# Two heads at a time in three attentions of a two-block transformer kernel: one head per half of the array, probabilities divided before the value product

## The chip, the cores and the metric

The kernel runs on one core of a Trainium2 chip. The metric is the device time of one execution in microseconds. Three runs of the kernel before took 2606.26, 2607.33 and 2609.94 us; the median is 2607.33 us. The core has a matrix engine (PE, with its weight loads shown apart as PEld), three engines for elementwise work (DVE, ACT and POOL), and queues that move data between the memory outside and the on-chip memory. PE writes into PSUM, which this kernel divides into eight tiles of 128 partitions by 512 fp32 values, called banks here.

## The reference

512 tokens of width 1024 pass through a first block of one layer and a second block of two layers. Each layer mixes tokens by several branches and then applies a feed-forward network. Three attentions matter here.

The first block has a sliding-window attention with 8 query heads of width 64 that share 2 key-value heads; a query sees the 128 latest keys, and a learned sink value is added to each denominator:

```python
scores = jnp.einsum('bnqhgd,bnkhd->bnhgqk', qb, kw)
logits = jnp.where(valid[None, :, None, None], scores + alibi, -jnp.inf)
m = jnp.maximum(logits.max(axis=-1), sink)
p = jnp.exp(logits - m[..., None])
denom = p.sum(axis=-1) + jnp.exp(sink - m)
o = jnp.einsum('bnhgqk,bnkhd->bnqhgd', p, vw) / jnp.moveaxis(denom, 4, 2)[..., None]
```

Each layer of the second block has an attention with 8 heads of width 64 in which a query sees only the 128 keys that an index picks. The index scores come from 4 heads of width 64; the bias of keys not chosen is a large negative number, and the rest is a plain softmax:

```python
rel = jax.nn.relu(jnp.einsum('bqhd,bsd->bqhs', qib.astype(jnp.float32), ki32))
score = jnp.einsum('bqh,bqhs->bqs', wib.astype(jnp.float32), rel)
_, idx = lax.top_k(score, topk)
logits = jnp.einsum('bqhd,bqkhd->bhqk', qb.astype(jnp.float32), k_sel) * scale
p = jax.nn.softmax(logits, axis=-1)
return jnp.einsum('bhqk,bqkhd->bqhd', p, v_sel).astype(q.dtype)
```

Beside each attention runs a chunked linear recurrence with 4 heads of width 128, and its output is merged with that of the attention.

## The kernel before

Activations are held as features by tokens: 8 tiles of 128 features by 512 tokens. A projection (`project`, lines 181 to 196) multiplies weight tiles of 128 by 128 with those tiles. Weights and activations are split into a high and a low part, so each weight tile takes three matmuls of 512 columns: lines 193, 194 and 195. In the profile their output is called mm. For each set of weights, one DMA, a cast on ACT (whi) and a subtraction on DVE or POOL (wlo) go ahead.

The other matmuls, whose output is called at, are plain fp32, and each is two PE instructions in the trace, except for a transpose, which is one. They write into PSUM banks of a lane: lane "a" (the attentions) and lane "h" (the recurrences) have two banks each (`BANKS`), and a tile takes the next bank of its lane when what lay there has been read.

The instruction order of each engine is not the order of the code. A scheduler takes what is ready by its own estimate of the times, so projection matmuls of the stages behind stand between the steps of an attention and of a recurrence head. Once placed, the order of an engine's queue is fixed; on DVE and ACT an instruction that waits holds up those behind it.

The window attention is `swa`. For each of the 4 query blocks of 128 tokens (n), it makes the scores of 8 heads with two PSUM tiles per four heads (line 552); a score product uses the 64 rows (partitions) in which its head lies, rows 0 to 63 or 64 to 127, and streams 256 keys (128 in the first block). DVE adds the bias and finds the maximum (line 558). For each pair of heads ACT takes the exponential and the sum (line 572), PE transposes the probabilities (line 575), ACT copies them (sPT, line 577), and PE multiplies them with the values (line 581): the transposed probabilities are the 128 by 128 stationary operand, 64 columns of values are streamed, and the output is tokens by features, all heads in one PSUM tile o. At the end of the block DVE multiplies by the reciprocal of the denominator (son, line 587), four transposes turn it to features by tokens (line 588, in the profile L239 of a helper), and `split_into` (lines 215 to 218) writes the high part on ACT and the low part on DVE.

The top-k attention is `dsa`. `select` computes index scores of four heads (line 867), weights and sums them, and finds the 128 largest of each row on DVE. `attend(i)` handles the query block i against i + 1 key blocks: for each of 8 heads one score product (line 917), bias and maximum (line 919), exponential (line 921), transposes (line 925), copy (aPT, line 927) and value products (line 929), all in tile o of the block; then the multiplication by the reciprocal (aon, line 933), four transposes and `split_into`. Since o stays for the whole block, scores and transposed probabilities share the other bank of the lane.

The recurrence heads (`hgrn_head`) run beside it in lane "h": level by level DVE and POOL update hf and hG, make lvx, and PE multiplies (lines 502 and 457).

## Time and profile before

| | |
|---|---|
| three runs, us | 2606.26, 2607.33, 2609.94 |
| profiled execution: span, us | 2605.2 |
| mean granted clock of PE | 0.993 of full speed |
| PE busy, us (share) | 2533.9 (97%) |
| PE weight loads, us (share) | 2040.0 (78%) |
| DVE busy, us (share) | 1355.5 (52%) |
| ACT busy, us (share) | 1000.8 (38%) |
| POOL busy, us (share) | 754.3 (29%) |

The page gives no other time of the profiled execution than its span, from its first to its last instruction. PE counts as busy while any matmul is in it, and matmuls overlap: one of 512 columns lasts 0.39 us by the trace, and the next starts 0.23 us after it. So a busy share near 100% does not show what an instruction really occupies; that is read from the distance between the starts.

### The profile page before, as it was taken

What the parts mean: (1) busy time and instruction counts of PE and PEld (TensorE: products, weight loads), DVE (VectorE), ACT (ScalarE), POOL (GpSimd) and SP (SyncE); (2) the same over time, 40 slices, a digit from 0 to 9 for tenths busy, and PEclk for the clock granted to TensorE, in tenths of its full rate; (3) what the DMA queues carried; (4) which work ended last, traced back from release to release, by engine and by line L of the source; (5) the groups of instructions that cost most, each with busy time, mean ns of one, the idle gap of its engine ahead of it and who ended that gap; (6) DMA issues with size and microseconds to landing.
All of it is one profiled execution on the core that took longest, in us unless ns stands there. A gap on an engine that the chain in (4) does not pass through costs nothing.

```text
span 2605.2 us, 31523 instructions
## 1 busy us (share of the span) xinstructions
PE 2533.9 (97%) x11742; PEld 2040.0 (78%) x11742; DVE 1355.5 (52%) x2568; ACT 1000.8 (38%) x1813; POOL 754.3 (29%) x640
## 2 busy tenths in 40 slices
PE   9999999999999997999999999999799999999999
PEld 7777888788888865777878888887577787888887
DVE  4565322477774579675244444336967524444432
ACT  5543333444443333553343333334354433433321
POOL 4234334511101234443351111013545435211100
PEclk9999999999999999999999999999899999999999
DMA  3112222222222221111322222322110122222232
GB/s 135 57 51 81 93 94 93 101 97 96 97 94 90 90 73 65 42 41 51 99 96 94 97 95 94 96 88 81 65 49 33 45 94 97 97 97 97 95 101 87
DMA packets 67434, 217.66 MB, mean 84 GB/s; under 512 B 7744, under 2 KB 8640, under 8 KB 67280
## 3 DMA queue, kind: packets, MB, share of 16 engines
q1 hardware_dynamic: 67280, 215.65, 24.9%
q8 instruction: 92, 1.51, 0.2%
q14 instruction: 62, 0.51, 0.1%
HBM read 213.52 MB, written 2.10 MB: 83 GB/s over the span
## 4 chain that ended last, share of the span: by engine, by line
PE 83%; DVE 12%; issue 2%; POOL 2%; ACT 1%; DMA 0%; SPq 0%; DVEq 0%; POOLq 0%; ACTq 0%
PE mm L194 24%; PE mm L195 24%; PE mm L193 24%; PE at L917 1%; PE mm L169 1%; PE mm L168 1%; PE mm L170 1%; DVE score L879 1%; PE at L929 1%; DVE m L878 1%; DVE wlo L152 1%; PE at L239 1%; DVE hf L490 1%; DVE rope L792 1%; DVE rsq_w L232 1%
## 5 line engine op out<-in xcount | busy, mean ns | idle before, releaser
L149 ACT CAST whi<-wraw 128x512 fp32r<-128x512 f32 (+3 forms) x824 | 502.2, 610 | 1177.7 <-PE mm L195 992.1
L194 PE MATMUL mm<-xl,whi 128*128 128x512 f32 x1920 | 757.2, 394 | 0.0
L193 PE MATMUL mm<-xh,wlo 128*128 128x512 f32 x1920 | 756.8, 394 | 0.0
L195 PE MATMUL mm<-xh,whi 128*128 128x512 f32 x1920 | 755.5, 393 | 0.0
L152 DVE TENSOR_TENSOR wlo<-wraw,whi 128x512 fp32r<-128x512 f32 (+1 forms) x529 | 387.4, 732 | 457.9 <-ACT whi L149 455.2
L152 POOL TENSOR_TENSOR wlo<-wraw,whi 128x512 fp32r<-128x512 f32 (+2 forms) x295 | 383.6, 1301 | 767.0 <-ACT whi L149 747.1
L194 PEld LDWEIGHTS mm<-xl,whi 128*128 128x128 f32 x1920 | 361.7, 188 | 79.8 <-issue 7.5
L195 PEld LDWEIGHTS mm<-xh,whi 128*128 128x128 f32 x1920 | 361.6, 188 | 78.2 <-issue 5.6
L193 PEld LDWEIGHTS mm<-xh,wlo 128*128 128x128 f32 x1920 | 361.5, 188 | 76.6 <-issue 3.5
L193 PE MATMUL mm<-acth,wlo 128*128 128x512 f32 x528 | 208.6, 395 | 0.0
L195 PE MATMUL mm<-acth,whi 128*128 128x512 f32 x528 | 208.6, 395 | 0.0
L194 PE MATMUL mm<-actl,whi 128*128 128x512 f32 x528 | 208.6, 395 | 0.0
L725 POOL TENSOR_TENSOR fg<-fg,rstd 128x512 f32<-128x512 f32 x44 | 56.7, 1289 | 426.1 <-ACT fg L724 426.1
L168 PE MATMUL mm<-wlo,xh 128*128 128x512 f32 (+2 forms) x384 | 146.6, 382 | 20.0 <-POOL wlo L152 12.4
L170 PE MATMUL mm<-whi,xh 128*128 128x512 f32 (+2 forms) x384 | 144.5, 378 | 0.0
L169 PE MATMUL mm<-whi,xl 128*128 128x512 f32 (+2 forms) x384 | 144.2, 375 | 0.2 <-DVE xl L281 0.2
L202 DVE TENSOR_TENSOR gate<-mm,rstd 128x512 f32<-128x512 f32 x56 | 38.7, 691 | 169.3 <-PE mm L195 169.3
L270 POOL TENSOR_TENSOR acc<-acc,sq 128x512 f32<-128x512 f32 x39 | 58.7, 1506 | 205.9 <-ACT sq L267 204.9
L195 PEld LDWEIGHTS mm<-acth,whi 128*128 128x128 f32 x528 | 99.0, 187 | 24.3
L193 PEld LDWEIGHTS mm<-acth,wlo 128*128 128x128 f32 x528 | 99.0, 187 | 24.2
L194 PEld LDWEIGHTS mm<-actl,whi 128*128 128x128 f32 x528 | 99.0, 187 | 24.2
L168 PEld LDWEIGHTS mm<-wlo,xh 128*128 128x128 f32 x384 | 73.5, 191 | 40.7 <-POOL wlo L152 15.7
(347 smaller groups left out, 3288.3 us busy)
## 6 DMA issues: line engine op xcount, KB each, us to landing
wraw<-in_w_ffn_in SPq DMA_DIRECT2D x88, 512.0 KB, 3.2
wraw<-in_w_gate SPq DMA_DIRECT2D x56, 512.0 KB, 3.2
wraw<-in_w_in SPq DMA_DIRECT2D x52, 512.0 KB, 3.2
wraw<-in_w_up SPq DMA_DIRECT2D x44, 512.0 KB, 3.2
wraw<-in_w_tok SPq DMA_DIRECT2D x32, 512.0 KB, 3.2
wraw<-in_w_ffn_out SPq DMA_DIRECT2D x32, 512.0 KB, 3.5
wraw<-in_w_down SPq DMA_DIRECT2D x16, 512.0 KB, 3.5
wraw<-in_w_po SPq DMA_DIRECT2D x32, 256.0 KB, 2.6
```

Of the source, the lines that this page charges most:

```text
L149: nc.scalar.copy(wh, raw[:, k:k + m, :])
L152: eng.tensor_tensor(wl, raw[:, k:k + m, :], wh.bitcast(F32), op=OP.subtract)
L168: nc.tensor.matmul(ps[t][:, 0:w], xh, wl, start=i == 0, stop=False)
L169: nc.tensor.matmul(ps[t][:, 0:w], xl, wh, start=False, stop=False)
L170: nc.tensor.matmul(ps[t][:, 0:w], xh, wh, start=False, stop=i == KD - 1)
L193: nc.tensor.matmul(ps, wl, xh, start=i == 0, stop=False)
L194: nc.tensor.matmul(ps, wh, xl, start=False, stop=False)
L195: nc.tensor.matmul(ps, wh, xh, start=False, stop=i == n - 1)
L202: self.nc.vector.tensor_tensor(out, ps, other, op=OP.mult)
L232: nc.vector.scalar_tensor_tensor(w, w, -0.5, y, op0=OP.mult, op1=OP.mult)
L270: (nc.vector if d % 2 and len(acc) > 1 else nc.gpsimd).tensor_tensor(a, a, sq, op=OP.add)
L725: nc.gpsimd.tensor_tensor(g, g, self.rstd, op=OP.mult)
```

## The change

The scores of two heads, one in rows 0 to 63 and one in rows 64 to 127, are issued one behind the other into two PSUM tiles, in `select` and `attend`; `swa` had that already. The reciprocal of the denominator is taken for each pair of heads, and the probabilities are multiplied by it before they are transposed. The value product changes its operands' roles in a new function `values_of`: 64 columns of values are the stationary operand, 128 columns of transposed probabilities are streamed, and the output is features by tokens, one head in output partitions 0 to 63 and the other in 64 to 127 of a PSUM tile that a pair has for itself. It goes to `split_into` at once; the multiplication of the output and its four transposes are left out.

```diff
@@ swa
-            o = self.at([P, 8, 64])
             for h2 in (0, 4, 2, 6):
-                pt = self.at([P, 2, 2, P])
+                dn = den[:, h2:h2 + 2]
                 for s in range(2):
                     hd = h2 + s
                     nc.scalar.activation(Ls[hd], Ls[hd], AF.Exp, scale=-1.0,
                                          bias=nm[:, hd:hd + 1], accum_out=den[:, hd:hd + 1])
+                nc.vector.tensor_tensor(dn, dn, es[:, h2:h2 + 2], op=OP.add)
+                nc.vector.reciprocal(dn, dn)
+                pt = self.at([P, 2, 2, P])
+                for s in range(2):
+                    hd = h2 + s
+                    nc.vector.tensor_scalar(Ls[hd], Ls[hd], den[:, hd:hd + 1], None, op0=OP.mult)
                     for kb in range(w // P):
                         nc.tensor.transpose(pt[:, s, kb, :], Ls[hd][:, kb * P:(kb + 1) * P], self.ident)
                 PT = self.u("sPT", shape=[P, 2, 2, P])
                 nc.scalar.copy(PT[:, :, 0:w // P, :], pt[:, :, 0:w // P, :])
-                for s in range(2):
...
-            nc.vector.tensor_tensor(den, den, es, op=OP.add)
-            nc.vector.reciprocal(den, den)
-            on = self.u("son", shape=[P, 8, 64])
-            nc.vector.tensor_tensor(on, o, den[:, :, None].to_broadcast([P, 8, 64]), op=OP.mult)
-            ps = self.transpose4(on.rearrange("p n c -> p (n c)"), None)
-            for m in range(4):
-                self.split_into(y[m], ps[:, m, :], slice(n * P, (n + 1) * P))
+                kv = slice(P + 64 * (h2 // 4), P + 64 * (h2 // 4) + 64)
+                self.values_of(y[h2 // 2], slice(n * P, (n + 1) * P), w // P, lambda s, kb: (
+                    skv[n + 1 - w // P + kb][:, kv], PT[:, s, kb, :]))
         return y
+
+    def values_of(self, y, c, n, operands):
+        o = self.at([P, P])
+        for kb in range(n):
+            for v in range(2):
+                lhs, rhs = operands(v, kb)
+                self.nc.tensor.matmul(o[64 * v:64 * v + 64, :], lhs, rhs, start=kb == 0, stop=kb == n - 1)
+        self.split_into(y, o, c)
@@ attend
+            for m in range(4):
+                ps = [self.at() for _ in range(2)]
+                L = [self.u("aL") for _ in range(2)]
+                for v in range(2):
+                    r = slice(64 * v, 64 * v + 64)
+                    nc.tensor.matmul(ps[v][:, 0:w], qT[i][r, m, :], kT[m][r, 0:w], start=True, stop=True)
+                for v in range(2):
+                    hd = 2 * m + v
+                    nc.vector.tensor_tensor_reduce(L[v][:, 0:w], ps[v][:, 0:w], bias[i][:, 0:w], -1.0, 3e38,
+                                                   op0=OP.add, op1=OP.min, accum_out=nm[:, hd:hd + 1])
+                    nc.scalar.activation(L[v][:, 0:w], L[v][:, 0:w], AF.Exp, scale=-1.0, bias=nm[:, hd:hd + 1],
+                                         accum_out=den[:, hd:hd + 1])
+                nc.vector.reciprocal(den[:, 2 * m:2 * m + 2], den[:, 2 * m:2 * m + 2])
+                PT = []
+                for v in range(2):
+                    hd = 2 * m + v
+                    nc.vector.tensor_scalar(L[v][:, 0:w], L[v][:, 0:w], den[:, hd:hd + 1], None, op0=OP.mult)
+                    pt = self.at([P, NT, P])
+                    for kb in range(i + 1):
+                        nc.tensor.transpose(pt[:, kb, :], L[v][:, kb * P:(kb + 1) * P], self.ident)
+                    PT.append(self.u("aPT", shape=[P, NT, P]))
+                    nc.scalar.copy(PT[v][:, 0:i + 1, :], pt[:, 0:i + 1, :])
+                self.values_of(y[m], slice(i * P, (i + 1) * P), i + 1, lambda v, kb: (
+                    av[kb][:, P * m + 64 * v:P * m + 64 * v + 64], PT[v][:, kb, :]))
```

In `select` the four index scores are issued in two pairs in the same way. What the scheduler makes of it is seen in the instruction orders. A row of them is a source line, the operation, output and operands by name, and the shape of the output, with a count.

The first place is PE at the second query block of the window attention (L552 scores, L575 and L580 transposes of the probabilities, L239 son those of the output, L593 value products of the change). Before:

```order
L239 MATMUL at<-csts,son 128x128 x4
L552 MATMUL at<-sk,sq 128x256 x2
L193 MATMUL mm<-xh,wlo 128x512
L194 MATMUL mm<-xl,whi 128x512
L195 MATMUL mm<-xh,whi 128x512
L193 MATMUL mm<-xh,wlo 128x512
L194 MATMUL mm<-xl,whi 128x512
L195 MATMUL mm<-xh,whi 128x512
L552 MATMUL at<-sk,sq 128x256 x4
L193 MATMUL mm<-xh,wlo 128x512
L552 MATMUL at<-sk,sq 128x256 x2
L575 MATMUL at<-csts,sL 128x128 x4
```

The same place in the change, on PE:

```order
L593 MATMUL at<-sPT,skv 64x128 x2
L552 MATMUL at<-sk,sq 128x256 x4
L194 MATMUL mm<-xl,whi 128x512
L552 MATMUL at<-sk,sq 128x256 x4
L195 MATMUL mm<-xh,whi 128x512
```

The eight scores stood in groups of 2, 4 and 2 and now stand in two groups of 4; the transposes of the output are gone.

The second place is PE in the top-k attention of the first layer, at two neighbouring steps of the second query block (L917 and L924 scores, L925 and L938 transposes, L929 and L593 value products). Before, one head:

```order
L925 MATMUL at<-csts,aL 128x128 x2
L195 MATMUL mm<-xh,whi 128x512
L193 MATMUL mm<-xh,wlo 128x512
L194 MATMUL mm<-xl,whi 128x512
L929 MATMUL at<-av,aPT 128x64 x2
L917 MATMUL at<-kT,qT 128x256
L195 MATMUL mm<-xh,whi 128x512
```

In the change, a pair of heads, on PE:

```order
L938 MATMUL at<-csts,aL 128x128 x2
L195 MATMUL mm<-xh,whi 128x512
L938 MATMUL at<-csts,aL 128x128 x2
L193 MATMUL mm<-xh,wlo 128x512
L593 MATMUL at<-aPT,av 64x128
L194 MATMUL mm<-xl,whi 128x512
L593 MATMUL at<-aPT,av 64x128 x3
L924 MATMUL at<-kT,qT 128x256
L195 MATMUL mm<-xh,whi 128x512
L193 MATMUL mm<-xh,wlo 128x512
L924 MATMUL at<-kT,qT 128x256
```

Of the four value products the first stands apart from the other three, and two projection matmuls stand between the two scores of the next pair.

The third place is DVE in the same attention of the change (L935 multiplies the probabilities, L931 is the reciprocal, L218 evicts the output of a pair, L490, L486 and L504 belong to a recurrence head):

```order
L931 RECIPROCAL aden<-aden 128x2
L486 TENSOR_TENSOR lvx<-hf,hq 128x32x8
L935 TENSOR_SCALAR aL<-aL,aden 128x256 x2
L490 TENSOR_TENSOR hf<-hf 128x32x8
L486 TENSOR_TENSOR lvx<-hf,hq 128x16x16
L504 COPY_PREDICATED AT<-masks,at 120x32x8
L490 TENSOR_TENSOR hf<-hf 128x16x16
L486 TENSOR_TENSOR lvx<-hf,hq 128x8x32
L218 TENSOR_TENSOR yal<-at,yah 128x128
```

The reciprocal and the multiplies are new between the steps of the recurrence, and the eviction of a pair's output stands behind five of these steps.

## Rows read from the trace of the kernel before

**Rows 1.** The page: busy time by engine, and the chain that ended last.

```profile
PE 2533.9 (97%) x11742; PEld 2040.0 (78%) x11742; DVE 1355.5 (52%) x2568; ACT 1000.8 (38%) x1813; POOL 754.3 (29%) x640
...
PE 83%; DVE 12%; issue 2%; POOL 2%; ACT 1%; DMA 0%; SPq 0%; DVEq 0%; POOLq 0%; ACTq 0%
```

**Rows 2.** Stretches: length, busy time (instructions) by engine, clock, DMA share, GB/s.

```profile
100.00:150.00 50.00, 48.05 (x300) 39.43 (x299) 30.84 (x101) 26.00 (x72) 8.93 (x9) 1.00 0.13 44
...
1100.00:1150.00 50.00, 49.73 (x297) 38.58 (x296) 36.88 (x89) 24.24 (x49) 26.56 (x32) 1.00 0.09 33
1500.00:1550.00 50.00, 50.00 (x222) 41.43 (x221) 22.01 (x33) 17.45 (x28) 5.39 (x5) 1.00 0.28 95
```

**Rows 3.** Timeline of PE, top-k attention: start, length (us), line, names, shapes, count.

```profile
1105.55 0.61 PE L239 MATMUL at<-csts,aon 128*128 128x128 f32 x4
1106.08 0.91 PE L917 MATMUL at<-kT,qT 64*128 64x384 f32 x2
1106.92 0.50 PE L194 MATMUL mm<-xl,whi 128*128 128x512 f32 x1
1107.26 0.40 PE L195 MATMUL mm<-xh,whi 128*128 128x512 f32 x1
1107.49 0.39 PE L193 MATMUL mm<-xh,wlo 128*128 128x512 f32 x1
```

**Rows 4.** Timeline of PE, products with 64 output columns.

```profile
1112.15 0.68 PE L457 MATMUL at<-lvx 128*64 128x64 f32 x8
1112.76 0.50 PE L195 MATMUL mm<-xh,whi 128*128 128x512 f32 x1
1113.09 0.39 PE L193 MATMUL mm<-xh,wlo 128*128 128x512 f32 x1
```

**Rows 5.** Timeline of PE, scores of the window attention.

```profile
78.88 0.71 PE L552 MATMUL at<-sk,sq 64*128 64x128 f32 x8
...
106.44 1.13 PE L552 MATMUL at<-sk,sq 64*128 64x256 f32 x4
...
109.31 1.14 PE L552 MATMUL at<-sk,sq 64*128 64x256 f32 x8
```

**Rows 6.** Timeline of PE, value products of the window attention and what follows.

```profile
97.12 1.00 PE L581 MATMUL at<-skv,sPT 128*128 128x64 f32 x8
97.95 0.61 PE L575 MATMUL at<-csts,sL 128*128 128x128 f32 x4
```

**Rows 7.** Groups by line, PE: count, busy us, mean ns, idle before.

```profile
L929 PE MATMUL at<-av,aPT 128*128 128x64 f32 x320 | 46.0, 275 | 0.0
L581 PE MATMUL at<-skv,sPT 128*128 128x64 f32 x112 | 14.9, 273 | 0.0
L457 PE MATMUL at<-lvx 128*64 128x64 f32 x96 | 8.3, 232 | 5.2 <-POOL lvx L440 3.5 <-DVE lvx L486 1.6
L239 PE MATMUL at<-csts,aon 128*128 128x128 f32 x32 | 4.9, 275 | 0.0
```

**Rows 8.** Groups by line and shape, DVE.

```profile
L933 DVE TENSOR_TENSOR aon<-at,aden 128x512 f32<-128x512 f32 x8 | 5.5, 682 | 2.4 <-PE at L929 2.4
L524 DVE TENSOR_SCALAR alibi<-csts 128x256 f32<-128x256 f32 x8 | 1.7, 286 | 0.0
L931 DVE RECIPROCAL aden<-aden 128x8 f32<-128x8 f32 x8 | 1.6, 202 | 2.5 <-ACT aL L921 2.5
L880 DVE TENSOR_SCALAR score<-score 128x512 f32<-128x512 f32 x2 | 0.9, 428 | 0.1
L749 DVE TENSOR_SCALAR angn<-ang 128x128 f32<-128x128 f32 x2 | 0.4, 222 | 0.0
```

**Rows 9.** Waits of PE: who waited for whom, us in total, times, longest.

```profile
PE at L239 <- DVE aro L817: 20.0, 8, 8.4
PE at L502 <- DVE lvx L486: 2.5, 5, 0.8
PE at L917 <- DVE yal L218: 1.6, 2, 1.0
```

More of the change, by code (lines that the diff above doesn't have):

```diff
@@ L863, in select @@
             sc = self.t("score")
-            for h in range(4):
-                r = slice(64 * (h % 2), 64 * (h % 2) + 64)
-                ps = self.at()
-                nc.tensor.matmul(ps[:, 0:w], iqT[i][r, h // 2, :], ikT[r, 0:w], start=True, stop=True)
-                rl = self.u("rel")
-                nc.scalar.activation(rl[:, 0:w], ps[:, 0:w], AF.Relu)
-                iwc = iw[:, i * 4 + h:i * 4 + h + 1]
-                if h == 0:
-                    nc.vector.tensor_scalar(sc[:, 0:w], rl[:, 0:w], iwc, None, op0=OP.mult)
-                else:
-                    nc.vector.scalar_tensor_tensor(sc[:, 0:w], rl[:, 0:w], iwc, sc[:, 0:w], op0=OP.mult, op1=OP.add)
+            for m in range(2):
+                ps = [self.at() for _ in range(2)]
+                for v in range(2):
+                    r = slice(64 * v, 64 * v + 64)
+                    nc.tensor.matmul(ps[v][:, 0:w], iqT[i][r, m, :], ikT[r, 0:w], start=True, stop=True)
+                for v in range(2):
+                    h = 2 * m + v
+                    rl = self.u("rel")
+                    nc.scalar.activation(rl[:, 0:w], ps[v][:, 0:w], AF.Relu)
+                    iwc = iw[:, i * 4 + h:i * 4 + h + 1]
+                    if h == 0:
+                        nc.vector.tensor_scalar(sc[:, 0:w], rl[:, 0:w], iwc, None, op0=OP.mult)
+                    else:
+                        nc.vector.scalar_tensor_tensor(sc[:, 0:w], rl[:, 0:w], iwc, sc[:, 0:w], op0=OP.mult, op1=OP.add)
             nc.vector.tensor_tensor(sc[:, i * P:w], sc[:, i * P:w], self.cst("unseen"), op=OP.add)
@@ L931, in attend @@
-            nc.vector.reciprocal(den, den)
-            on = self.u("aon", shape=[P, 8, 64])
-            nc.vector.tensor_tensor(on, o, den[:, :, None].to_broadcast([P, 8, 64]), op=OP.mult)
-            ps = self.transpose4(on.rearrange("p n c -> p (n c)"), None)
-            for m in range(4):
-                self.split_into(y[m], ps[:, m, :], slice(i * P, (i + 1) * P))
+            for m in range(4):
+                ps = [self.at() for _ in range(2)]
+                L = [self.u("aL") for _ in range(2)]
+                for v in range(2):
+                    r = slice(64 * v, 64 * v + 64)
+                    nc.tensor.matmul(ps[v][:, 0:w], qT[i][r, m, :], kT[m][r, 0:w], start=True, stop=True)
+                for v in range(2):
+                    hd = 2 * m + v
[5 more added lines that the diff above has]
+                PT = []
+                for v in range(2):
+                    hd = 2 * m + v
[7 more added lines that the diff above has]
+                    av[kb][:, P * m + 64 * v:P * m + 64 * v + 64], PT[v][:, kb, :]))
```

23 lines of the change are left out of this document (removed).

## The prediction

> **What bounds the kernel now.** I read the page first: PE is busy 97% of a span of 2605.2 us and the chain that ended last is PE for 83% of its length [rows 1]. The reader is to see that nothing else is near: DVE has 52%, ACT 38%. A busy PE can still hide waits, so the table by stage came next [rows 2]. Sliding-window attention lies in 78 to 145 us, the two top-k attentions in about 1034 to 1204 and 1889 to 2060; around them PE is as full (48.05 and 49.73 of 50 us) as in the plain feed-forward stretch (50.00). There the scheduler fills PE with projection matmuls (mm) while an attention waits for DVE and ACT. So an attention costs what its own instructions occupy on PE, plus stalls where the filler runs out; the latency of its chain is mostly covered. Third, the timeline of PE alone, to see what occupies it.
>
> **A price that no busy time shows: changing the shape of the array.** A score product uses 64 rows of the array, a projection all 128. From 1105.55 to 1107.26 us, 1.71 us, stand four transposes, one score product (two instructions of 384 columns) and one projection matmul [rows 3]. A pitch of 128 columns is 0.107 us: eight score instructions of 128 columns, run two at a time, last 0.71 us, eight of 256 last 1.14, and the 0.43 between is four times 128 columns [rows 5]. So the work is 0.43 + 0.64 + 0.23 (the pitch of the last two projection rows) = 1.30 us; 0.41 us are left, 0.2 for entering the 64-row shape and 0.2 for leaving it. A product with 64 output columns (L457) shows the same: 0.94 us from its start to the second projection behind it, for 0.50 of its own (eight at (0.68 - 0.23)/7 = 0.06) and 0.23 of projection leaves 0.21 [rows 4, 7]. In that sum lies the first weight load, which nothing covers; with 64 columns it is half as long, so I take 0.15 for entering a column shape (0.1 to 0.2).
>
> **The change part by part.**
> *Value product.* Before, head and key block cost two instructions that load 128 columns and stream 64: 0.83 us for eight, 0.104 each [rows 6], 0.42 per pair of heads and key block. Now one head fills the left 64 columns of the array, the other the right, and 128 columns are streamed: 0.107 per instruction. If the two run beside each other, a pair and key block cost 0.215, half. There are 80 of these in the top-k attentions (320 instructions before) and 28 in the window attention (112) [rows 7]: 108 x 0.215 = 23.2 us less. In the new order 21 value blocks start with a lone product and a projection matmul follows; each gives one unit of 0.215 back: 4.5. Left: -18.7 us. The trace has no two column halves at work at once, so the bounds are 0 (they run one after the other) and -18.7. The nearest row is the row shape: eight instructions for both row halves take 1.14 us where four for one half take 1.13 [rows 5], full overlap. I take -18.7.
> The Trainium skill ("TensorE: Matmul & The Clock Gate", Measured speedup vs the span model) gives three column tiles 2.38 times the speed; by it too this term would be near its full size, and no run here shows it yet.
> *Transposes of the output.* 32 fewer in the top-k attentions [rows 7] and four for each of the window attention's four blocks, 48 at 0.107: -5.2 us.
> *Scores.* "Back to back" does not come true in the top-k attentions. The lane has two PSUM banks, and the pair's output now takes the one that the next pair's second score needs; that score waits until ACT and DVE have evicted the output, and the order puts one to three other rows between the two scores in 28 of 32 pairs. They keep their own entry and exit and overlap nothing. The four adjacent pairs may gain up to 3.4 us; since the second waits for the bank, I take 1. The index scores stood in fours before. The window attention gains: for each of three query blocks the order had 2, 4, 2 score products, and the twos used one half twice; now it has 4 and 4. One unit of 0.86 us each: -2.6 us.
> *Changes of shape.* Counted over the whole order: entries into the row shape 81 to 74, into the column shape 12 to 81, back to the full array 91 to 121. That is 0.2 x (-7) + 0.15 x 69 + 0.2 x 30 = +15 us (12 to 18). This is the price of the change, and it eats most of what the halves save.
> *DVE.* 96 multiplies of the probabilities at 0.22 to 0.43 by width (0.29 at 256, 0.43 at 512) [rows 8]: 20.6 + 8.7 us; reciprocals and sums per pair instead of per block +9; the multiplications of the output go (12 at 0.68): -8.3. Net +30 us, on an engine at 62 to 74% in these stages [rows 2]. PE's filler hides it as long as it lasts. What is new is a wait: in the DVE queue the multiplies wait for both heads' exponentials, and behind them stand the subtractions that free PSUM and the head updates of the recurrence (lvx, hf), for which PE's L502 products wait. Today these waits are small: 2.5 us behind lvx, 1.6 behind yal; the 20 us behind aro lie before the attention [rows 9]. Bounds: -3 (the pair chain is shorter than two head chains) to +20 (0.4 us for each of 48 pairs); taken, near today's: +4.
> *Sum.* -18.7 - 5.2 - 1 - 2.6 + 15 + 4 = -8.5 us: a span of 2596.7. The page gives the execution no other time than its span; the median of the three timed runs, 2607.33, lies 2.1 above it. Predicted: 2599.
>
> **A rule against it.** The first rows of the eight-fold group show the overlap at its full size whatever the order of the two halves in the queue: 1.14 for eight against 1.13 for four. The Trainium skill (same page, What overlaps and what doesn't) says that matmuls keep strict order in start and end. By that each of the 69 value blocks would lose one instruction of 0.107, since a product is two instructions and the partner's first could not pass the second. For row halves the trace disagrees; for column halves no run shows it.
>
> **The rivals.**
> 1. *The column halves do not overlap.* The first term is 0: span 2605.2 + 10.2 = 2615.4, median 2617. For it: only one column half is ever seen at work; its two streams come from all 128 partitions at once, which those of two row halves never do. Against it: the overlap of row halves is complete.
> 2. *The normalisation is the new wait (the other side again, with the halves overlapping).* Place: the DVE queue in the attentions, where an eviction or an lvx stands behind a multiply that waits for ACT. It decides from 12.5/48 = 0.26 us of extra stall for a pair (the sum without its +4); at 0.7 us a pair, the length of one lvx or hf step, the span is 2605.2 - 12.5 + 33 = 2626, median 2628; at half of it 2611.
> 3. *The halves overlap, but each block's matmuls start in the order of the queue.* Each of the 69 blocks is longer by one instruction, 69 x 0.107 = +7.4: span 2604, median 2606, no change. Against it: eight row-half scores end no later than four [rows 5].
> 4. *The waits shrink.* Fewer, longer steps per pair and an attention that ends one recurrence head earlier (in the new order its last value product comes before the last head's level products): waits -8 instead of +4, span 2585, median 2587.
>
> **How the numbers follow.** Forecast 0.50, its own range 2590 to 2609; rival 1 0.20; rival 2 0.13; rival 3 0.05; rival 4 0.12. A difference of 0.2%, 5.2 us, is what a measurement of this kernel can tell: faster means under 2602.1, slower over 2612.5. The forecast gives 0.32 faster, 0.15 same, 0.03 slower; rival 1 0.05 same and 0.15 slower; rival 2 0.02 and 0.11; rival 3 0.01 faster and 0.04 same; rival 4 0.12 faster. Together 0.45, 0.26, 0.29. The range, 2584 to 2620, holds rivals 1, 3 and 4 and half of rival 2.
>
> **What the changed profile would show.** Value instructions (L593): a row of eight lasting about 0.11 + 0.43 + 0.17 = 0.7 us says that the halves overlap, 1.1 us that they do not. From the last value instruction to the score behind it a gap of 0.1 us with an uncovered load. 48 transposes fewer under L239. DVE about 30 us busier. PE idle behind DVE lvx and DVE yal still a few us in the table of waits; if these grow to 15 us or more, rival 2 decided. If the scores L924 are seen in overlapping pairs, my reading of the bank is wrong. The forecast is wrong if the stretches outside the attentions change, since nothing in them does.

## The result, and the profile after

The kernel after takes 2626.28 us (median of 4 runs, 2624.96 to 2629.91), the kernel before 2607.44 (4 runs): a ratio of 1.0073, 95% interval 1.0059 to 1.0087. It is slower by 18.8 us, where 8 us less were forecast and the range ended at 2620. The profiled execution is the slowest of the four: its span is 2628.1 us, 22.9 more than the span of before, and what follows accounts for these 22.9; the clock and the waits of the median execution were not split, and it is 3.6 us shorter.

First the page of the kernel after, busy time by engine and the chain that ended last, which answers to [rows 1]:

```profile
PE 2538.2 (97%) x11694; PEld 2022.7 (77%) x11694; DVE 1393.4 (53%) x2700; ACT 994.4 (38%) x1807; POOL 753.5 (29%) x640
...
PE 80%; DVE 13%; issue 2%; POOL 2%; ACT 1%; DMA 0%; SPq 0%; DVEq 0%; POOLq 0%; ACTq 0%
```

48 instructions fewer on PE, DVE busier by 38 us (30 were forecast), and nothing that looks like a new bound. PE is even 4.3 us busier with less to do. The stretches of the kernel after (length, busy time and instructions by engine, granted clock, DMA share, GB/s) say more [rows 2]:

```profile
100.00:150.00 50.00, 46.38 (x271) 33.69 (x270) 34.05 (x120) 24.98 (x70) 8.69 (x8) 0.86 0.10 33
1100.00:1150.00 50.00, 47.40 (x262) 32.87 (x262) 33.13 (x88) 21.75 (x48) 17.15 (x20) 0.93 0.09 32
1500.00:1550.00 50.00, 50.00 (x222) 41.41 (x221) 21.86 (x33) 16.88 (x28) 6.46 (x5) 1.00 0.29 95
```

In the two attention stretches PE does 29 and 35 instructions fewer in the same 50 us, and the column of the clock, 1.00 in [rows 2], reads 0.86 and 0.93. The feed-forward stretch is as it was. The value products themselves do what was forecast. PE in the timeline of the kernel after (start, length, line, names, shapes, count), which answers to [rows 4, 6]:

```profile
1090.23 0.43 PE L593 MATMUL at<-aPT,av 128*64 128x128 f32 x2
1090.59 0.50 PE L194 MATMUL mm<-xl,whi 128*128 128x512 f32 x1
1091.03 0.65 PE L593 MATMUL at<-aPT,av 128*64 128x128 f32 x6
1091.61 0.70 PE L924 MATMUL at<-kT,qT 64*128 64x256 f32 x2
```

The row of six is not three pairs: since one product stands apart, four of its instructions belong to one half and two to the other, and by their single starts in the trace (1091.03 twice, 1091.19 twice, 1091.30, 1091.41) the two run beside the four. A full row of eight, in the window attention of the same kernel, shows it plainly:

```profile
119.05 0.66 PE L593 MATMUL at<-sPT,skv 128*64 128x128 f32 x8
119.64 0.33 PE L580 MATMUL at<-csts,sL 128*128 128x128 f32 x1
```

It lasts 0.66 us (about 0.7 was forecast for overlap, 1.1 without), and the next instruction starts 0.59 after its start. One after the other the eight would need 8 x 0.107 = 0.86; in twos they need 0.43, and the rest is entering and leaving the column shape. PE's waits in the kernel after (who waited for whom, us in total, times, longest), beside [rows 9]:

```profile
PE at L239 <- DVE aro L820: 20.2, 8, 8.4
...
PE at L239 <- POOL hG L508: 6.7, 4, 2.1
...
PE at L239 <- DVE ron L408: 5.7, 8, 1.3
PE at L430 <- DVE gD L427: 5.4, 4, 2.1
PE at L938 <- DVE aL L935: 4.2, 6, 0.9
...
PE at L502 <- DVE lvx L486: 2.6, 4, 0.7
...
PE at L924 <- DVE yal L218: 2.1, 2, 1.4
```

Two of them in the kernel before:

```profile
PE at L430 <- DVE gD L427: 3.3, 3, 1.1
PE at L239 <- DVE ron L408: 3.0, 6, 1.0
```

The waits behind lvx and yal, the only two that the prediction priced, hardly moved (2.5 to 2.6, 1.6 to 2.1). Those that grew have other names: hG (no row in the kernel before) and ron, which belong to the recurrence; gD, to the first block's recurrence; and aL, the multiply that the change brought in (4.2; the transposes of before waited 1.5 for the exponential).

**Where 22.9 us came from.** No view gives it, so I worked it out from the trace. For each PE instruction I took the distance to the next start and subtracted its price at full clock (0.23 us for a projection row, 0.107 per 128 columns, 0.1 for each change of shape). More than 0.12 us above it counts as a wait; where the granted clock is at the lower of its two levels (1.2 GHz instead of 2.4), up to once the price again counts as half clock; the rest is PE's own work. Between the first and the last PE instruction, in us:

| stretch | own work | waits | half clock |
|---|---|---|---|
| start to end of the window attention's stage, 292 us | 266.5 to 262.4 | 19.8 to 23.0 | 6.1 to 10.9 |
| attention and recurrence, layer 1, 190 us | 181.9 to 177.5 | 8.7 to 18.2 | 0.0 to 3.0 |
| the same, layer 2 | 181.9 to 178.7 | 9.3 to 17.3 | 0.0 to 2.9 |
| all the rest | 1871.4 to 1871.7 | 49.0 to 51.5 | 5.4 to 5.7 |
| **whole** | **-11.4** | **+23.2** | **+11.0** |

So the saving is there (-12.5 was forecast without the waits); the waits, forecast at +4, took 23; and the clock, for which the sum had no term, took 11. By the same split, with a head counted from its first product to the next head's, the waits of layer 1's fourth recurrence head rose from 2.5 to 6.5 us, those of its third from 1.2 to 3.3, and those at the attention's own products from 1.8 to 5.7.

**Where the clock falls.** PE in the kernel after, timeline around 125 us (in brackets the idle time before, and who ended it):

```profile
122.70 0.40 PE L195 MATMUL mm<-xh,whi 128*128 128x512 f32 x1
125.24 0.80 PE L430 MATMUL at<-gE,gD 128*128 128x128 f32 x4 [2.14 <-DVE gD L427]
125.97 1.12 PE L593 MATMUL at<-sPT,skv 128*64 128x128 f32 x8
127.03 2.83 PE L552 MATMUL at<-sk,sq 64*128 64x256 f32 x8
129.79 0.79 PE L430 MATMUL at<-gE,gD 128*128 128x128 f32 x2
...
135.95 0.63 PE L193 MATMUL mm<-xh,wlo 128*128 128x512 f32 x1
136.38 0.63 PE L194 MATMUL mm<-xl,whi 128*128 128x512 f32 x1
```

A wait of 2.14 us, and behind it everything takes up to twice as long (the pitch of projection rows is 0.43 us, where it was 0.23), until 139.4. The kernel e2 below has the same 1394 PE instructions in the same order up to the end of this stage. Its timeline at the same place:

```profile
122.05 0.40 PE L195 MATMUL mm<-xh,whi 128*128 128x512 f32 x1
124.58 0.71 PE L430 MATMUL at<-gE,gD 128*128 128x128 f32 x4 [2.13 <-DVE gD L427]
125.22 0.66 PE L593 MATMUL at<-sPT,skv 128*64 128x128 f32 x8
125.81 1.89 PE L552 MATMUL at<-sk,sq 64*128 64x256 f32 x8
127.63 0.49 PE L430 MATMUL at<-gE,gD 128*128 128x128 f32 x2
```

The same wait, and this time the clock stays. Each kernel has one profile; of the seven with this order, three show 13.7 us at half clock here (after, e5, e6), e8 shows 3.4, and e2, e4 and e15 show none. In the eight profiles with the order of before (before, e1, e7, e10 to e14) there is none between 64 and 160 us, and no such wait:

```profile
123.03 0.38 PE L430 MATMUL at<-gE,gD 128*128 128x128 f32 x2
```

Busy time hides this: a PE at half clock is busy for twice as long. The stretches of before, of after and of e2:

```profile
110.00:125.00 15.00, 14.58 (x94) 12.08 (x90) 10.44 (x33) 10.74 (x29) 4.44 (x5) 1.00 0.11 37
```

```profile
110.00:125.00 15.00, 12.02 (x73) 8.33 (x72) 14.52 (x40) 10.50 (x29) 6.10 (x6) 1.00 0.16 50
125.00:140.00 15.00, 14.76 (x56) 11.09 (x57) 7.73 (x32) 5.62 (x20) 0.98 (x1) 0.54 0.06 22
```

```profile
125.00:140.00 15.00, 14.32 (x103) 11.21 (x102) 10.95 (x48) 7.25 (x25) 1.28 (x1) 1.00 0.05 13
```

After: 56 instructions in 14.76 busy us at a clock of 0.54; e2: 103 in 14.32. The first lines name the reason for the wait as well: from 110 to 125 us DVE is busy 14.52 of 15 us, where it had 10.44. Here the added DVE work is not hidden; gD stands in a full queue. That the division fills it is seen in e3 and e9, which leave the division out: DVE is then busy for 6.24 of these 15 us (e3), the longest wait for gD is back at 1.1 us, as in before, and there is no half clock at this place. PE's waits in e3:

```profile
PE at L430 <- DVE gD L427: 3.4, 3, 1.1
```

In the attention stages the clock fell at the end of waits of 1.4 to 2.1 us too (1119, 2044 and 2081 us); behind the wait of 1.79 us shown next (1216.77) it did not.

**Where the recurrence lost its cover.** Cover is what PE can do for one chain while the other keeps it waiting; a recurrence head with no product of the attention beside it is called bare. The last recurrence head of layer 1, PE in the kernel before and then after:

```profile
1196.48 0.65 PE L457 MATMUL at<-lvx 128*64 128x64 f32 x8 [0.83 <-DVE lvx L486]
1197.06 0.50 PE L193 MATMUL mm<-xh,wlo 128*128 128x512 f32 x1
1197.40 1.00 PE L929 MATMUL at<-av,aPT 128*128 128x64 f32 x8
1198.33 1.12 PE L917 MATMUL at<-kT,qT 64*128 64x512 f32 x2
1199.38 0.66 PE L239 MATMUL at<-csts,hG 128*128 128x128 f32 x4
```

```profile
1207.91 1.02 PE L502 MATMUL at<-lvx 128*120 128x64 f32 x8 [0.74 <-DVE lvx L486]
...
1209.76 0.97 PE L502 MATMUL at<-lvx 128*112 128x64 f32 x8 [0.54 <-DVE lvx L486]
...
1214.33 0.65 PE L457 MATMUL at<-lvx 128*64 128x64 f32 x8 [0.29 <-DVE lvx L486]
1216.77 0.66 PE L239 MATMUL at<-csts,hG 128*128 128x128 f32 x4 [1.79 <-POOL hG L508]
```

Before, a value product and a score of the attention stand between the head's products, and PE comes to hG when it is done. After, the attention's last product is at 1174 us instead of 1204, the order has nothing between L457 and L239, and PE stands still for 1.79 us. Waits behind the attention's last product in layer 1: 1.2 us before, 9.7 after.

### The profile page after: what moved, and what is told of

Same layout as the page of the kernel before. It is cut to its first block, busy times and chain, and to the rows that moved or that the text cites. A ratio compares the mean times of both kernels' runs of the same rounds, so it can differ in the third digit from the quotient of the medians.

```text
span 2628.1 us, 31547 instructions
## 1 busy us (share of the span) xinstructions
PE 2538.2 (97%) x11694; PEld 2022.7 (77%) x11694; DVE 1393.4 (53%) x2700; ACT 994.4 (38%) x1807; POOL 753.5 (29%) x640
## 4 chain that ended last, share of the span: by engine, by line
PE 80%; DVE 13%; issue 2%; POOL 2%; ACT 1%; DMA 0%; SPq 0%; DVEq 0%; POOLq 0%; ACTq 0%
PE mm L195 23%; PE mm L194 23%; PE mm L193 23%; PE at L924 1%; DVE score L885 1%; DVE m L884 1%; PE at L593 1%; PE mm L169 1%; PE mm L168 1%; PE mm L170 1%; DVE wlo L152 1%; PE at L239 1%; DVE rope L795 1%; DVE rsq_w L232 1%; POOL hG L488 1%
## 5 line engine op out<-in xcount | busy, mean ns | idle before, releaser
L195 PEld LDWEIGHTS mm<-acth,whi 128*128 128x128 f32 x528 | 99.0, 187 | 24.2
L194 PEld LDWEIGHTS mm<-actl,whi 128*128 128x128 f32 x528 | 99.0, 187 | 24.2
L193 PEld LDWEIGHTS mm<-acth,wlo 128*128 128x128 f32 x528 | 99.0, 187 | 24.2
L168 PEld LDWEIGHTS mm<-wlo,xh 128*128 128x128 f32 x384 | 73.6, 192 | 43.5 <-POOL wlo L152 16.3
```

The lines of the kernel that those rows point to most:

```text
L168: nc.tensor.matmul(ps[t][:, 0:w], xh, wl, start=i == 0, stop=False)
L193: nc.tensor.matmul(ps, wl, xh, start=i == 0, stop=False)
L194: nc.tensor.matmul(ps, wh, xl, start=False, stop=False)
L195: nc.tensor.matmul(ps, wh, xh, start=False, stop=i == n - 1)
```

## The experiments

Eighteen kernels ran, each against runs of the kernel before on the same chip. The first fifteen were chosen and their expectations written while I knew only of waits; the split that shows the clock came after them, and the last three test it. The table gives for each the ratio to before with its interval, and from its profiled execution the whole program's own work, waits and half clock, split as above.

| kernel | median us | ratio [95%] | own | waits | half clock |
|---|---|---|---|---|---|
| before | 2607.44 | | 2501.7 | 86.8 | 11.5 |
| after | 2626.28 | 1.0073 [1.0059, 1.0087] | 2490.3 | 110.0 | 22.5 |
| e1 | 2623.71 | 1.0055 [1.0043, 1.0068] | 2494.0 | 104.8 | 17.9 |
| e2 | 2611.78 | 1.0009 [1.0000, 1.0017] | 2497.9 | 88.1 | 15.3 |
| e3 | 2627.06 | 1.0070 [1.0057, 1.0084] | 2493.0 | 114.0 | 13.1 |
| e4 | 2621.82 | 1.0056 [1.0044, 1.0069] | 2489.7 | 106.0 | 18.4 |
| e5 | 2634.35 | 1.0094 [1.0080, 1.0108] | 2489.3 | 107.5 | 32.3 |
| e6 | 2622.14 | 1.0051 [1.0039, 1.0064] | 2485.5 | 108.9 | 20.7 |
| e7 | 2589.79 | 0.9923 [0.9910, 0.9937] | 2458.4 | 106.3 | 17.6 |
| e8 | 2595.36 | 0.9948 [0.9936, 0.9960] | 2451.9 | 116.1 | 20.3 |
| e9 | 2625.18 | 1.0070 [1.0054, 1.0086] | 2489.7 | 104.3 | 22.2 |
| e10 | 2535.12 | 0.9717 [0.9705, 0.9730] | 2384.2 | 126.1 | 17.5 |
| e11 | 2622.73 | 1.0047 [1.0035, 1.0059] | 2489.1 | 107.1 | 15.8 |
| e12 | 2626.31 | 1.0066 [1.0054, 1.0078] | 2488.5 | 107.5 | 23.4 |
| e13 | 2628.17 | 1.0074 [1.0060, 1.0088] | 2501.6 | 101.4 | 17.6 |
| e14 | 2622.67 | 1.0050 [1.0037, 1.0062] | 2486.2 | 110.9 | 16.3 |
| e15 | 2622.18 | 1.0051 [1.0039, 1.0064] | 2478.6 | 106.5 | 27.0 |
| e16 | 2610.38 | 1.0008 [0.9999, 1.0017] | 2498.6 | 93.5 | 10.9 |
| e17 | 2623.81 | 1.0052 [1.0039, 1.0066] | 2466.1 | 124.4 | 26.0 |
| e18 | 2625.91 | 1.0069 [1.0057, 1.0082] | 2476.8 | 121.4 | 20.1 |

**e1 and e2: the two halves of the change.** e1 has the top-k attentions of after with the `swa` of before; e2 the reverse. The core of e1 against after:

```diff
-                self.values_of(y[h2 // 2], slice(n * P, (n + 1) * P), w // P, lambda s, kb: (
-                    skv[n + 1 - w // P + kb][:, kv], PT[:, s, kb, :]))
+                for s in range(2):
...
+                        nc.tensor.matmul(o[:, hd, :], PT[:, s, kb, :],
...
+            nc.vector.tensor_tensor(on, o, den[:, :, None].to_broadcast([P, 8, 64]), op=OP.mult)
```

> The change in the top-k attentions (attend, select) alone; the window attention stays as before. Cover theory (the loss is the top-k attention ending about one recurrence head early, after which that head's chain on DVE and POOL is bare): most of the loss stays, about 2622 us, between the change's 2626 and 4 us less. DVE theory (multiplies and reciprocals in the DVE queue hold up everything): the loss is spread by the added DVE time, 20 us in top-k against 10 in the window, so about 2620. Shape theory (changes of array shape cost more than 0.15 to 0.2 us each): 48 of the window's shape changes less of 92 more, so about 2617.

> The change in the window attention alone; the top-k attentions stay as before. Cover theory: 2610 to 2612 us (PE waits in that stage grew by 6 us, its occupancy fell by 3). DVE theory: about 2614. Shape theory: about 2617.

Both came as expected: +15.2 and +3.2 us against their own runs of before, together 18.4, the whole change. The eleven runs of e2 go from 2607.47 to 2614.16, and their mean clocks go with them: 2607.5 to 2609.1 in four runs at 0.991, 2612.8 to 2613.9 in three at 0.988 or 0.989 (the four at 0.990 lie anywhere, 2608.4 to 2614.2). The window part of the change goes with the clock. Seven kernels here share its order up to the end of that stage (after, e2, e4, e5, e6, e8, e15), with own work of 262.3 to 262.7 us and waits of 22.3 to 24.8; at 5.4 to 5.6 us of half clock the stage takes 290.6 to 290.8 us, at 7.2 to 10.9 it takes 293.3 to 296.4. The kernel before needs 292.3, and the eight kernels with its order there 290.6 to 293.3.

**e3: no division.** The reciprocals, the sums and the multiplies of the probabilities are left out:

```diff
-                nc.vector.reciprocal(den[:, 2 * m:2 * m + 2], den[:, 2 * m:2 * m + 2])
-                    nc.vector.tensor_scalar(L[v][:, 0:w], L[v][:, 0:w], den[:, hd:hd + 1], None, op0=OP.mult)
```

> The change without the division by the denominators in all three attentions (sum with the sink, reciprocals and multiplies left out, so the probabilities stay undivided): DVE loses 96 multiplies and 48 reciprocals. Cover theory: the attentions end as early or earlier and the last recurrence head is still bare; only the waits behind the multiplies (about 6 us) go: 2615 to 2622 us, waits of PE behind POOL hG and DVE ron stay. DVE theory: nearly all of the 30 us of new waits goes: about 2597 us. Shape theory: 2624.

The theory that the division alone is the new wait falls: without it the time is the same, 5 us above the range that cover gave. Its waits tell why:

```profile
PE at L239 <- DVE ron L408: 8.1, 11, 1.3
PE at L239 <- POOL hG L508: 8.1, 6, 1.9
PE at L502 <- DVE lvx L486: 5.9, 12, 0.7
```

The attention's own waits went (5.7 to 1.2 us in layer 1), the attention then ended at 1134 us, two recurrence heads stood bare instead of one, and the recurrence's waits rose from 9.9 to 16.1.

**e10, e7 and e8: what a bare head costs.** Blocks of the attention are left out, the values copied in their place: all four of before (e10), the last of before (e7), the last of after (e8).

```diff
-                attend("abcd".index(c))
+                if c != "d":                      # e7, e8; e10 copies for every block
+                    attend("abcd".index(c))
+                else:
+                    for m in range(4):
+                        self.split_into(y[m], got["av"][3][:, m * P:(m + 1) * P], slice(3 * P, 4 * P))
```

> The kernel BEFORE with all four query blocks of both top-k attentions left out (values are copied in their place): nothing stands beside the recurrence heads but projections. By the order PE's own work falls by 114 us. Cover theory: four bare heads in each layer at 6.4 us, 25 us of waits at the recurrence in a layer against 4.8, so 2531 us, not 2495. If a bare head waits no more than a covered one: 2495 us or a little less.

> The kernel BEFORE, with the fourth query block of both top-k attentions left out (values are copied in its place). By the order, PE's own work falls by 41 us. Cover theory: the last recurrence head is bare in each layer as in the change, and its waits rise by 4 to 5 us: 2576 us. Chain theory (in the kernel before nothing is wrong with the cover): the whole work falls away, 2567 us or a little less.

> The CHANGE with the fourth query block left out in the same way. By the order, PE's own work falls by 37 us against the change. Cover theory: the attention ends still earlier and about one more head in each layer is bare: 2626 - 37 + 9 = 2598 us, so 22 us over the kernel before with the same block left out. Chain theory: 16 blocks' pairs fewer, a quarter of the new waits goes too: 2584 us.

In e10 PE's work falls by 117.5 us and the time by 74. PE's waits in e10:

```profile
PE at L239 <- POOL hG L508: 11.5, 8, 1.8
PE at L502 <- DVE lvx L486: 10.1, 16, 0.7
PE at L239 <- DVE ron L408: 9.3, 12, 1.0
```

They come at the same places in each of the eight heads: 24.2 us of waits for four heads in layer 1, 6.1 for one, against 4.8 for all four where an attention stands beside them. In e7, 43 us less of PE's work bring 20 us. Other kernels give the same price: by the split, the twenty bare heads of e10, e3, e7, e8 and after wait 4.8 to 6.7 us each. This is the clearest result here: **work of the attention is the cover of the recurrence, and what is taken from it comes back in part as waits.** e8's time came near its figure; in e7 even less arrived than cover said (2576 expected). So the second figure of e8's expectation missed: e8 is 5.6 us slower than e7, not 22. The change costs 18.8 us while the kernel before has its cover, and 5.6 once both lack it; a quarter of the change is gone there too, so that this comparison alone does not show the cause.

**e4, e5, e6 and e9: give the last head its cover back.** The attention's blocks are issued later, so that they lie beside other heads (e4: the last block with the third head's code; e5: one block behind each of the first two heads and two behind the third; e6: two, one, one; e9: e6 without the division, as in e3).

```diff
+            for i in {0: (0, 1,), 1: (2,), 2: (3,)}.get(hd, ()):      # e6; e5: {0: (0,), 1: (1,), 2: (2, 3,)}
+                with self.on("a"):
+                    self.attend(i)
```

> The change, with the fourth query block of each top-k attention put into the program after the third recurrence head, so that it runs beside the fourth. Nothing is left out. Cover theory: the waits in the bare tail (10 to 11 us in each layer) shrink by two thirds: about 2612 us. DVE theory and shape theory: the same DVE work and as many shape changes (125 returns to the full array against 121), so 2626.

> The change, with the first query block of each top-k attention put into the program after the first recurrence head, the second after the second, the third and fourth after the third, so that in the instruction order an attention step stands beside every head up to the end. Nothing is left out. Cover theory (each recurrence head that runs without an attention beside it costs 6.4 us of PE waits, against 2 us beside one): the tail's 9 us in each layer go, 2608 us, and PE waits behind POOL hG and DVE ron fall from 12.4 us to under 5. Chain theory (the waits are made by the pair's own longer chain, wherever it stands): 2624 us, with the waits now at L938 and L924.

> The change, with the first and second query blocks after the first recurrence head, the third after the second, the fourth after the third. Nothing is left out. Its order has 261 changes of array shape, 15 fewer than the change. Cover theory: 2605 us (18 us from the tail and 3 us from the shapes). Chain theory: 2621 us.

> The blocks of e6_blocks_spread and the division by the denominators left out as in e3_no_norm. Two-part theory (waits at the attention's own products come from its longer pair chain, waits at the recurrence's products from missing cover, and each goes with its cause): waits at the attention under 2 us in each layer, at the recurrence 7 to 10 since its order still leaves the fourth head mostly bare: 2612 us. Conserved-wait theory (a wait removed in one place comes back whole in the other): 2622 us.

All four missed what cover alone would give; e6 came out at the figure of the chain theory. In e4 the waits of the fourth head fell from 6.5 to 3.3 us in layer 1, but the attention still ended at 1199 us, the start of the third head was left nearly bare (3.3 us of waits, as in after), and the attention's waits rose from 5.7 to 6.8. In e5 the recurrence's waits in layer 1 did fall, from 9.9 to 5.0 us, but the attention's rose from 5.7 to 8.4 and half clock cost 10.1 us in that layer alone, the most of any kernel; e5 is the slowest of all. In e9 the attention's waits fell to 1.8 and 1.6 us in the two layers, as expected, but the recurrence's were 12.8 and 11.4, where 7 to 10 were expected. So cover is a cause, but not one that can be bought back by placing alone.

**e11 and e12.** e11 is e6 with the `swa` of before; e12 is e11 with the multiply of each pair's second head on ACT:

```diff
+                    if v:
+                        nc.scalar.activation(L[v][:, 0:w], L[v][:, 0:w], AF.Copy, scale=den[:, hd:hd + 1])
+                    else:
```

> e6_blocks_spread with the window attention of the kernel before; nothing is left out. The two attentions' parts add (e1 and e2 did): 2622 less 3 = 2619 us on either theory; 2622 if the window's part depends on the rest.

> e11_spread_old_window with the multiply of the second head of each top-k pair on ACT instead of DVE, so that the two multiplies of a pair run side by side; nothing is left out. Two-part theory: the waits at the transposes (L938, 5.1 and 3.7 us) shrink by half: 2614 us. If the DVE queue's other work decides: 2619 us or, with ACT the later engine, more.

e11 came out at e6's time, within the intervals: the window part changed nothing there. e12 was slower than e11, against the expectation: 4 to 6 us off DVE in each layer, no less waiting, and 7.6 us more of half clock in the profiled executions, which lie 7.4 us apart (the medians 3.6).

**e13, e14 and e15: separate the division from the pairs.** e13 keeps the heads one after the other as in before, with the division ahead of the transposes and the two column halves. In e14 (on e13) and e15 (on after) the value products of the late head are issued first:

```diff
# e13, in attend: one head after the other
+                    ps = self.at()
+                    nc.tensor.matmul(ps[:, 0:w], qT[i][r, m, :], kT[m][r, 0:w], start=True, stop=True)
...
+                    nc.vector.reciprocal(den[:, hd:hd + 1], den[:, hd:hd + 1])
# e14, e15, in values_of
-            for v in range(2):
+            for v in (1, 0):
```

> The window attention of the kernel before; in the top-k attentions the value products of the change, one head per half, and its division, but the steps of a pair's two heads in turn as before (scores, exponential, reciprocal, multiply, transposes, copy of the one, then of the other), so that the attention lasts as long as before. Nothing is left out. Its order has 286 changes of array shape and 4 us more PE work than the kernel before. Cover theory: the waits at the recurrence fall back to about 5 to 6 us in a layer although every multiply is still there, those at the attention stay near 4: 2609 + 4 + 4 = 2617 us. If the division itself makes the waits: 10 us or more at the recurrence or the attention in each layer as in the change, 2609 + 4 + 22 = 2635 us.

> e13_heads_in_turn with the second head's value product first in each block, so that a block waits once, for the later copy, and is no longer split in the order: 222 changes of shape, 17 us less PE work than e13 and 13 us less than the kernel before. Nothing is left out. Cover theory: waits as in e13, so 2609 - 13 + 6 = 2602 us, faster than the kernel before. If waits give back whatever PE saves: 2617 us, as e13.

> The change with the second head's value product first in each block, nothing else. Its order has 233 changes of shape instead of 276 and 11 us less PE work. Price of the shapes as forecast and waits unchanged: 2615 us. If the attention's earlier end takes it back: 2622 us or more.

e13's time fits neither figure, but it takes the two sorts of waits apart. Its attention lasts until the recurrence's end, the recurrence's waits are back at 2.9 us in layer 1 (4.8 before), and the division shows by itself, in PE's waits of e13:

```profile
PE at L940 <- DVE aL L937: 13.7, 19, 2.3
```

So the division does cost about 9 us in a layer (the attention's waits are 10.9 in layer 1, 1.8 before) where the heads go in turn; in after it costs less, since pairs give it time, and the bare head costs the rest. e14 and e15 save 15.4 and 11.7 us of PE's work against e13 and after, and gain 5.5 and 4.1 (e15 5.3, each against its own runs of before): most of it went into waits and half clock. e14, for which cover gave 2602 us, came out 14 us slower than before.

**e16: hold the clock.** e2 with a product of 512 columns ahead of L430 in each head of the first block's recurrence, its result overwritten:

```diff
+        nc.tensor.matmul(ps.rearrange("p n c -> p (n c)"), E[:, 0:P], self.csts[:, 0:T], start=True, stop=True)
```

> The kernel before with the window attention of the change, and in each of the four heads of the first block's recurrence one more product of 512 columns (two instructions, 0.85 us, its result overwritten) ahead of L430, in the stretch in which PE waits 2.3 us for DVE gD. Clock theory: the runs of the same kernel without it differ (2607.5 to 2614.2, mean clock 0.991 to 0.988) since PE falls to half clock behind that wait in some of them and not in others; with the wait broken up the clock stays up, all runs lie together near 2609 (2607.5 and up to 2 us of the added products that nothing hides), and the stretch around 125 us shows a granted clock of 1.00. Rival, the waits alone cost the time and the clock is a symptom: the added 4 x 0.85 us come on top of the old median, 2613 to 2615, and the spread stays.

The stretches of e16 at the place shown above:

```profile
110.00:125.00 15.00, 11.73 (x73) 7.99 (x72) 14.53 (x37) 9.66 (x26) 6.05 (x6) 1.00 0.22 70
125.00:140.00 15.00, 14.93 (x110) 11.76 (x109) 11.35 (x47) 7.75 (x25) 1.39 (x1) 1.00 0.04 11
```

The scheduler put the product further ahead, so the wait before gD stayed (2.19 us idle); the clock stayed up behind it all the same, as it does in three profiles without the product. Eight of eleven runs show a mean clock of 0.993 or 0.994, above each of e2's, and three 0.990. So half clock is no mere other name for the wait. But the time is e2's within the intervals: 4.4 us of half clock less, 5.4 of waits and 0.7 of work more. Among e16's own runs the three at 0.990 took 2611.7 to 2613.0 us and the eight others 2606.5 to 2611.6. That holding the clock makes the kernel faster than e2 is not shown.

**e17 and e18: free the bank early.** The wait ahead of the half clock at 1119 us in after was L924 behind yal, for the bank that the pair's output holds. e18 copies that output out by ACT before it is split; e17 does so on e15.

```diff
-        self.split_into(y, o, c)
+        x = self.u("ax", shape=[P, P])
+        self.nc.scalar.copy(x, o)
+        self.split_into(y, x, c)
```

> The change with the late half first (2622.2), and the pair's output copied out of PSUM by one ACT instruction before it is split, so that its bank no longer waits for DVE yal. In the run without the copy, waits of 1.7 to 1.9 us of L924 behind yal stand directly ahead of two of the stretches at half clock in the attention stages, and the half clock costs 12 us there in all. Clock theory: these waits go, half or more of the 12 us with them: 2612 to 2616. Rival, the total of the waits is given: 2620 or more.

> The change (2626.3) with the same copy by ACT and nothing else. Clock theory: the wait of 1.5 us of L924 behind yal ahead of the half-clock stretch at 1119 us goes, and 3 us of half clock in that layer with it; with 1 to 2 us of waits in each layer 2620 to 2623. Rival, the total of the waits is given: 2625 or more.

The wait for yal is gone from both tables of waits, PE's work fell by another 12.5 and 13.5 us, and the times are those of e15 and after: in e18 the attention ended earlier still, at 1160 us, and the recurrence's waits in layer 1 rose to 15.4 us. Half clock hardly moved (27.0 to 26.0 and 22.5 to 20.1), so the waits for these banks were not what kept the clock down. The times are those of the rival, that the waits take back what work gives.

**What the table shows as a whole.** From e13 to e17, PE's own work in the kernels with the change falls by 35.5 us, waits and half clock together rise by 31.4, and the time moves by 4. Layer 1's attention stage lasts 194.9 to 203.9 us in the fourteen kernels that have the change or a variant of it there with all four blocks; where PE works 167.1 us of it (e17) it lasts 198.4, and where PE works 181.7 (e13) 199.4. Before, PE worked 181.9 in 190.5. PE's work no longer sets that stage. No version that leaves nothing out was faster than the kernel before.

## Why the prediction was wrong, point by point

- **The value product (-18.7), the transposes, the scores and the changes of shape (+15): right as a sum.** The halves overlap and no instruction of a block is lost, which settles rivals 1 and 3. Against before, PE's own work fell by 4.1, 4.4 and 3.2 us in the three stages, 11.4 in all, where -12.5 was forecast; the terms were not measured one by one. A slip was in them: by the prediction's own 0.104 us for an instruction of before, 108 blocks save 21.7 us and not 23.2, which makes its sum -7.0 and the forecast without the waits -11.0. The groups of the kernel after give the counts of [rows 7]:

```profile
L593 PE MATMUL at<-aPT,av 128*64 128x128 f32 x320 | 34.8, 286 | 0.4
L593 PE MATMUL at<-sPT,skv 128*64 128x128 f32 x112 | 10.1, 298 | 0.0
```

- **The order: right.** The scores L924 do not stand in overlapping pairs in the top-k attentions, and the work outside the attentions is as it was (from the end of the window attention's stage to the first input product of layer 1, 593.1 and 593.2 us; from the end of layer 1's attention stage to that of layer 2, 527.0 in both). Only layer 2's input stage took 3.1 us longer, 1.6 of them half clock.
- **"DVE ... net +30 us": about right** (38). "PE's filler hides it as long as it lasts" was wrong in the window stage, where DVE reached 14.52 of 15 us; the 50 us slices of [rows 2] were too coarse to see a queue that fills for 15.
- **The step that failed is the term for new waits, "taken, near today's: +4".** Measured: +23.2 of waits and +11.0 of half clock. The term was mis-sized, and its bound of +20 too low. Three things were missing from it. It priced only lvx and yal, where the change's own steps touch the recurrence, and not the cover that the attention gives all the recurrence's products (e10, e7). It took the new chain through exponential, reciprocal and multiply as hidden by PE's filler; e13 shows its wait by itself. And it priced a wait at its own length, while the clock can make it longer. How much of the 23.2 is which is not fixed: removing one makes another grow (e3, e17). So the size of the term is measured, while its causes are shown singly and not as a sum.
- **Rival 4 had the observation and the wrong sign.** It saw that the attention would end "one recurrence head earlier" and expected 8 us less waiting. Ending earlier is what left that head bare.
- **Rival 2 had the sign and the wrong mark.** Its sign of recognition was lvx and yal at 15 us or more; they reached 4.7. The division is part of the cause, but leaving it out (e3) gives nothing back as long as the attention then ends earlier.

What stays open: what sets the 195 to 200 us of the stage, since DVE is busy for only 143 of layer 1's 199 and ACT and POOL for less; the order of each queue is fixed by the scheduler's own estimates, and an order made with measured durations was not tried. Open too is how far the clock is a cause in the attention stages, since e16 held it in the window stage alone and won nothing that can be told from noise.

## What to carry to other kernels

Where two chains share an engine, one is the other's cover. Before taking work from one, measure the other bare (here 6.1 us of waits for a recurrence head, the mean of layer 1 in e10, where the attention is left out; 4.8 to 6.7 for single heads), and count that as the price of every stretch in which the cover ends; giving the cover back by another order did not win the price back here (e4, e5, e6). And when a busy engine's instruction count falls while its busy time doesn't, look at the granted clock in narrow stretches before explaining it by waits.

## What the runs showed of the hardware

- Products in different 64-column halves run beside each other in fp32, as those in the row halves do: eight instructions of 128 columns in 0.59 us to the next start, entry and exit included (after, 119.05 us), where one after the other they would need 0.86.
- One wait of 2.14 us (PE was busy for 12.02 of the 15 us up to 125) was followed by 13.7 us at 1.2 GHz, and in a kernel with the same order up to there by none (after and e2, around 125 us). The cost there is 5.0 us by the split, more than twice the wait.
- Freeing a bank sooner (e17, e18) cut PE's own work by 12.5 and 13.5 us (changes of the array's shape fell from 233 to 203 and from 276 to 231), and not the time.
